# Second normalisation: the last token half's mean from row sums of the down weights and the gated values, its variance from squares summed by bank on ScalarE

## The chip, the cores and the metric

The kernel runs on one core of a Trainium2 chip. The metric is the device time of one execution in microseconds. A core has TensorE (PE), VectorE (DVE), ScalarE (ACT) and GpSimd (POOL), each with its own stream of instructions that it runs in order, and DMA queues fed from SyncE and GpSimd. The engines wait for one another by semaphores.

## The reference

A decoder layer over 256 tokens of 1024 features: a mixer, a normalisation, a gated MLP with a short convolution, and a second normalisation, which is the subject here.

```python
def layer_norm(x, g, b):
    xf = x.astype(jnp.float32)
    mu = xf.mean(-1, keepdims=True)
    var = jnp.square(xf - mu).mean(-1, keepdims=True)
    return ((xf - mu) * lax.rsqrt(var + LN_EPS) * g + b).astype(x.dtype)

def conv_gated_mlp(x, w_up, conv_ffn, w_down):
    u = causal_dwconv(jnp.einsum("bsd,df->bsf", x, w_up), conv_ffn)
    g, up = jnp.split(u, 2, axis=-1)
    return jnp.einsum("bsf,fd->bsd", jax.nn.silu(g) * up, w_down)
...
        x = layer_norm(ALPHA * x + mix, ln1_g[l], ln1_b[l])
        ffn = conv_gated_mlp(x, w_up[l], conv_ffn[l], w_down[l])
        x = layer_norm(ALPHA * x + ffn, ln2_g[l], ln2_b[l])
```

D_FF is 2816, that is 22 tiles of 128 features (NF). All is float32 to the outside.

## The kernel before

**Precision.** Each matrix product is made of three TensorE products. `split_into` (L87) cuts an operand into a high part (a cast on ScalarE, L89) and the rest (a subtraction on VectorE, L90); high times high, high times low and low times high are added up in PSUM.

**Order.** `chunk_order` lists the weight chunks (128x2048 each, one DMA each); `run` goes through them in that order. At step s it runs `elem_work` (L417): the evacuation left by step s-1, and in the places marked `None` of that list (or behind it) the halves of the split of the weights of step s+2. Then it starts a load, and issues the matmuls of step s. Every engine's stream is thus written out by hand: what stands in it is not moved by a scheduler. The MLP's steps are up 0 to 3, then dn 0, up 4, up 5, dn 1, up 6, up 7 and so on to dn 7, up 18, up 19, and at the end up 20, up 21, dn 8, dn 9, dn 10.

**An up step** gives one gated tile i of 128 features by 256 tokens. Its evacuation has two parts (`up_evac`). `conv` scales the result on ScalarE (L1104, two instructions) and adds the two older taps on VectorE (L1108, four). `gate` applies Silu on ScalarE (L1115), multiplies on VectorE (L1116), and splits the product into hh (L89, ScalarE) and hl (L90, VectorE). The list is `[conv, None, None, gate]`, so the two halves of a weight split stand between `conv` and `gate` on both engines. `up 0` and `up 1` are done token by feature and transposed back; their evacuation stands with that of up 2.

**A down step** dn d uses the gated tiles 2d and 2d+1 against the weight rows of the same features and adds into PSUM banks: for token half 0 two banks of 512 columns, for token half 1 one of 512 (bank 0) and two of 256 (banks 1 and 2). Steps 0 to 7 do both halves. Step dn 8 does all the rest of token half 0 (tiles 16 to 21, in this order), dn 9 bank 0 of half 1, dn 10 banks 1 and 2 (L1160 to L1171). A down step leaves no evacuation before dn 8.

**The second normalisation.** For each bank `ln_part` (L1000) adds the residual on VectorE (L1004) into the tile r of this token half and takes the statistics of it (`bn_stats`, L1005). For half 0 `ln_scale` makes mean and variance (L1013), and GpSimd raises the variance to -1/2 (L1014); `ln2_out` centres and multiplies by the gain (L1180), then scales and adds the bias (L1185) in two pieces of 512 columns, each followed by its DMA to the output. For half 1 this is in `finish` (L1188): the statistics are aggregated on VectorE (L1192), ScalarE takes the root (L1193; its table is loaded ahead of time at L1173), beside it VectorE centres (L1180), then takes the reciprocal (L1182) and does the last two passes.

Of the kernel before, what the change touches and what calls it, by code (L numbers as in the profile page):

```python
# [69 lines left out]
class Kernel:  # L70
# [1021 lines left out]
    def up_evac(self, i, get_ps):  # L1092
# [18 lines left out]
        def gate():  # L1111
            cu = st["cu"]
            hh = pp.tile([P, S], F32R, tag="hh", name=f"hh{i}", bufs=6)
            hl = pp.tile([P, S], F32R, tag="hlo", name=f"hl{i}", bufs=6)
# [1 line left out]
            v.tensor_mul(cu[:, 0, :], cu[:, 0, :], cu[:, 1, :])  # L1116
# [4 lines left out]
        return [conv, gate]

    def step_dn(self, s, d, *a):
        if d == 0:
# [6 lines left out]
        def mm(dd, kk, t, ps, cols):  # L1131
# [10 lines left out]
            for i, (left, right) in enumerate(((hh, wh), (hh, wl), (hl, wh))):  # L1142
                for lo, hi in parts[i]:
                    self.nc.tensor.matmul(ps[:, lo - a:hi - a], left, right[:, lo:hi], start=k == i == 0,  # L1144
                                          stop=k == NF - 1 and i == 2)

        def part(t, q):
            ps, cols = self.acc[t][q]
            self.ln_part(self.st[t], self.x1[:, t, :], ps, cols)
# [26 lines left out]
    def ln2_out(self, t):
        nc, st = self.nc, self.st[t]
        r, mv, rs = st["r"], st["mv"], st["rs"]
        v, (gain, bias) = nc.vector, self.lnrow
        v.scalar_tensor_tensor(r, r, mv[:, 0:1], gain, op0=ALU.subtract, op1=ALU.mult)  # L1180
        if t == 1:
            v.reciprocal(rs, rs)  # L1182
# [95 lines left out]
```

## Time and profile before

| what | value |
|---|---|
| median of 3 runs | 483.68 us (483.47 to 484.09) |
| the profiled execution's own time | 483.75 us |
| its span, first to last instruction | 481.9 us |
| instructions | 9733 |
| start of the MLP's first matmuls of dn 0 | 316.76 us |
| start of the last matmul | 474.51 us |
| start of the last pass of VectorE | 477.41 us |
| last output DMAs (two), issued from | 478.19 us |

Times in the traces count from the span's start. A row of the timeline has the start, the length, the engine, the line, the operation, output and inputs, and a count; rows of equal instructions are merged, so that the length of a merged row runs from the first start to the last end. In brackets stands idle time of the engine just before, and what ended it. A row of the view by groups has the busy time, the mean length in ns, and the idle time before. The names in it are those of the program's tiles: `raw` a chunk of weights as loaded, `wh` and `wl` its two parts, `cu` an up step's working tile, `ffn` the down product's banks, `ps_up` an up step's result.

### The profile page before, as it was taken

The page shows a single profiled execution, that of the slowest core. Times are in us where ns is not written, and L with a number is a line of the kernel's source. Part 1 is how long each engine was busy: PE and PEld are TensorE (multiplying, and loading weights), DVE is VectorE, ACT ScalarE, POOL GpSimd, SP SyncE. Part 2 cuts the span into 40 slices and gives each one's busy share as a digit, 9 for nine tenths or more (in the row PEclk, how much of TensorE's full clock was granted, in tenths as well). Part 3 has the DMA queues.
Part 4 walks back from the last instruction along what each step waited for, and adds up shares of the span by engine and source line. Part 5 has one row for each costly group of instructions (what it writes and reads, how often), then busy time and mean ns, then how long its engine had stood idle before and what let it go on. Part 6 is the DMA issues. An engine that isn't in the chain of part 4 may idle for free.

```text
span 481.9 us, 9733 instructions
## 1 busy us (share of the span) xinstructions
PE 473.1 (98%) x4016; PEld 464.8 (96%) x4016; DVE 368.9 (77%) x663; ACT 287.6 (60%) x487; POOL 30.2 (6%) x45
## 2 busy tenths in 40 slices
PE   8999999999999999999999999999999999999994
PEld 5999999999999999999999998999999999999993
DVE  4889985769676977785877788988768766776876
ACT  5686866585758665865764622767456544654540
POOL 0610011010100010002000001000000000000000
PEclk9999999999999999999999999999999999999998
DMA  7967646625663456424964491827464545455202
GB/s 262 386 253 210 216 176 211 260 89 174 222 234 126 141 217 235 164 94 175 356 252 174 179 346 34 308 97 262 175 218 175 209 186 192 173 214 209 88 1 87
DMA packets 18749, 93.76 MB, mean 195 GB/s; under 512 B 4593, under 2 KB 4857, under 8 KB 8849
## 3 DMA queue, kind: packets, MB, share of 16 engines
q1 hardware_dynamic: 14402, 86.82, 49.2%
q0 software_dynamic: 4160, 6.07, 4.2%
q8 instruction: 31, 0.51, 0.4%
q10 hardware_dynamic: 144, 0.26, 0.2%
q14 instruction: 12, 0.10, 0.1%
HBM read 92.05 MB, written 2.63 MB: 196 GB/s over the span
## 4 chain that ended last, share of the span: by engine, by line
PE 97%; DMA 1%; DVE 1%; SPq 0%; DVEq 0%; ACT 0%; issue 0%
PE ffn L1144 12%; PE ps_up L116 8%; PE ps_up L118 8%; PE ps_up L117 8%; PE ps_vm L116 2%; PE ps_vm L117 2%; PE ps_vm L118 2%; PE mix L118 2%; PE ps_wa L116 2%; PE ps_wb L116 2%; PE ps_ga L117 2%; PE ps_qb L116 2%; PE ps_gb L117 2%; PE ps_vb L117 2%; PE ps_qm L117 2%; PE ps_ga L116 2%
## 5 line engine op out<-in xcount | busy, mean ns | idle before, releaser
L90 DVE TENSOR_TENSOR wl<-raw,wh 128x1024 fp32r<-128x1024 f32 x150 | 176.6, 1220 | 28.2 <-ACT wh L89 28.1
L89 ACT CAST wh<-raw 128x1024 fp32r<-128x1024 f32 x150 | 149.6, 1052 | 4.6 <-DMA raw<-in_wst_dram 3.0
L117 PE MATMUL ps_up<-x1l,wh 128*128 128x256 f32 x320 | 88.3, 276 | 0.0
L118 PE MATMUL ps_up<-x1h,wl 128*128 128x256 f32 x320 | 88.3, 276 | 0.0
L116 PE MATMUL ps_up<-x1h,wh 128*128 128x256 f32 x319 | 88.1, 276 | 0.0
L117 PEld LDWEIGHTS ps_up<-x1l,wh 128*128 128x128 f32 x320 | 60.1, 188 | 0.0
L118 PEld LDWEIGHTS ps_up<-x1h,wl 128*128 128x128 f32 x320 | 60.1, 188 | 0.0
L116 PEld LDWEIGHTS ps_up<-x1h,wh 128*128 128x128 f32 x319 | 59.9, 188 | 0.0
L1108 DVE SCALAR_TENSOR_TENSOR cu<-ps_up,vec,cu 128x255 f32<-128x255 f32 (+1 forms) x80 | 33.0, 476 | 22.8 <-ACT cu L1104 22.8
L1144 PE MATMUL ffn<-wl,hh 128*128 128x256 f32 (+1 forms) x170 | 37.9, 280 | 0.0
L1144 PE MATMUL ffn<-wh,hl 128*128 128x256 f32 (+1 forms) x171 | 37.9, 280 | 0.0
L1144 PE MATMUL ffn<-wh,hh 128*128 128x256 f32 (+1 forms) x171 | 37.8, 279 | 0.0
L89 ACT CAST hh<-cu 128x256 fp32r<-128x256 f32 x22 | 8.9, 407 | 43.2 <-DVE cu L1116 43.2
L1104 ACT ACTIVATE cu<-ps_up,vec 128x256 f32<-128x256 f32 x40 | 16.7, 470 | 25.1 <-PE ps_up L118 25.1
L1144 PEld LDWEIGHTS ffn<-wh,hh 128*128 128x128 f32 x171 | 27.6, 188 | 0.3
L1144 PEld LDWEIGHTS ffn<-wh,hl 128*128 128x128 f32 x171 | 27.6, 188 | 0.3
L1144 PEld LDWEIGHTS ffn<-wl,hh 128*128 128x128 f32 x170 | 27.5, 188 | 0.2
L116 PE MATMUL mix<-wh,mgh 128*128 128x256 f32 x64 | 17.8, 279 | 0.0
L1014 POOL TENSOR_TENSOR rs<-mv,mhalf 128x1 f32<-128x1 f32 x3 | 3.0, 1000 | 235.7 <-DVE mv L1013 235.7
L117 PE MATMUL ps_vm<-wl,xth 128*128 128x256 f32 x64 | 17.8, 278 | 0.0
L116 PE MATMUL ps_qb<-xth,wh 128*128 128x256 f32 x64 | 17.8, 277 | 0.0
L116 PE MATMUL ps_wa<-yah,wh 128*128 128x256 f32 x64 | 17.8, 277 | 0.0
(312 smaller groups left out, 1439.1 us busy)
## 6 DMA issues: line engine op xcount, KB each, us to landing
raw<-in_wst_dram SPq DMA_DIRECT2D x77, 1024.0 KB, 4.9
rawr<-in_wst_dram SPq DMA_DIRECT2D x9, 256.0 KB, 5.7
lnrow<-in_rows_dram POOLq DMA_DIRECT2D x4, 512.0 KB, 6.0
rawr<-in_wst_dram SPq DMA_DIRECT2D x3, 512.0 KB, 5.6
band<-table POOLq DMA_DIRECT2D x4, 384.0 KB, 13.7
toe<-band POOLq DMA_DIRECT2D x4, 256.0 KB, 3.5
xtok<-in_x_dram POOLq DMA_DIRECT2D x1, 1024.0 KB, 5.2
out_dram<-r SPq DMA_DIRECT2D x4, 256.0 KB, 2.0
```

Of the source, the lines that this page charges most:

```text
L89: self.nc.scalar.copy(wh, raw)
L90: self.nc.vector.tensor_sub(wl, raw, wh.bitcast(F32))
L116: mm(ps, ah if first is None else first, bh, start=start, stop=False)
L117: mm(ps, ah, bl, start=False, stop=False)
L118: mm(ps, al, bh, start=False, stop=stop)
L1014: nc.gpsimd.tensor_tensor(st["rs"], st["mv"][:, 1:2], self.mhalf[:, 0:1], op=ALU.pow)
L1104: act.activation(cu[:, j, :], ps[:, j, :], AF.Copy, scale=tap(2, j))
L1108: v.scalar_tensor_tensor(cu[:, j, o:], ps[:, j, :S - o], tap(t, j), cu[:, j, o:], op0=ALU.mult, op1=ALU.add)
L1144: self.nc.tensor.matmul(ps[:, lo - a:hi - a], left, right[:, lo:hi], start=k == i == 0, stop=k == NF - 1 and i == 2)
```

## The change

The mean of a token over the 1024 outputs is known before the last matmul: the sum over columns of the down product is the sum over features of the gated value times the row sum of the down weights. The change computes token half 1's mean in this way.

- Each time the weights of a down step are split, ScalarE sums their rows: two ACTIVATE instructions (Copy, 128x1024, with an accumulator, `rows`), one for each of the two tiles of 128 features. Their output goes to the tile r of token half 0 (`st2[0]["r"]`) as scratch, the sums go to `wsum`. They are behind the evacuation list, so behind `gate` where the step before was an up step.
- The gated product is written to a tile of its own, `hf` (six buffers), not in place into `cu`. GpSimd multiplies its token half 1 by the row sum and adds it to `hsum` (`rowsum`; 22 products and 21 additions, 128x128).
- Behind bank 0 of token half 1 a small matmul adds `hsum` over the features (`ps_mu`, two columns). `x1_sum` sums the residual once on ScalarE and scales it on VectorE; `centre_known` puts the two together into the negative mean.
- For each bank `centre` adds the residual on VectorE, squares the centred values with an accumulator on ScalarE, and centres and multiplies by the gain on VectorE. The statistics (L1005, L1192) and the wide centring (L1180) of token half 1 are gone. `finish` adds up the first two banks' sums, takes the root with the third bank's sum as input and bias, and the reciprocal; the last passes are as before.

```diff
+        if self.order[s][0] == "dn":
+            d = self.order[s][1]
+            if d == 0:
+                self.st2 = [self.ln_tiles(f"2_{t}") for t in range(2)]
...
+            def rows():
+                for i, c in enumerate(cuts):
+                    k = 2 * d + i
+                    self.nc.scalar.activation(self.st2[0]["r"], c[2], AF.Copy, accum_out=self.wsum[:, k:k + 1])
+            return [lambda c=c: self.split_into(*c) for c in cuts] + [rows]
...
-            v.tensor_mul(cu[:, 0, :], cu[:, 0, :], cu[:, 1, :])
-            self.split_into(hh, hl, cu[:, 0, :])
+            hf = pp.tile([P, S], F32, tag="hf", name=f"hf{i}", bufs=6)
+            v.tensor_mul(hf, cu[:, 0, :], cu[:, 1, :])
+            self.split_into(hh, hl, hf)
+            self.hidf[i] = hf[:, P:]
...
+        def rowsum(dd):
+
+            for k in (2 * dd, 2 * dd + 1):
+                h, w = self.hidf.pop(k), self.wsum[:, k:k + 1].to_broadcast([P, P])
+                g.tensor_tensor(h if k else self.hsum, h, w, op=ALU.mult)
+                if k:
+                    g.tensor_tensor(self.hsum, self.hsum, h, op=ALU.add)
...
+            rowsum(d)
...
+            if d == 3:
+                self.evac[s] = self.x1_sum
...
             if d == d0 + 1:
-                self.nc.scalar.activation(self.st[1]["rs"], self.ident[:, 0:1], AF.Sqrt)
-                self.evac[s] = [lambda: part(1, 0)]
+                self.psmu = self.ps_main("ps_mu").rearrange("p a b -> p (a b)")[:, 0:2]
+                nc.tensor.matmul(self.psmu, self.hsum, self.mhalf, start=True, stop=True)
+                nc.scalar.activation(self.st[1]["rs"], self.ident[:, 0:1], AF.Sqrt)
+                self.evac[s] = [self.centre_known, lambda: self.centre(0)]
+
+    def x1_sum(self):
+        v, x = self.nc.vector, self.tiny[:, 0:1]
+        self.nc.scalar.activation(self.st[1]["r"], self.x1[:, 1, :], AF.Copy, scale=ALPHA, accum_out=x)
+        v.tensor_scalar(x, x, -1.0 / D, None, op0=ALU.mult)
+
+    def centre_known(self):
+
+        t = self.tiny
+        self.nc.vector.scalar_tensor_tensor(t[:, 1:2], self.psmu[:, 0:1], 2.0 / D, t[:, 0:1], op0=ALU.mult,
+                                            op1=ALU.add)
+
+    def centre(self, q):
...
+        v.scalar_tensor_tensor(r, self.x1[:, 1, c], ALPHA, ps, op0=ALU.mult, op1=ALU.add)
+        nc.scalar.activation(ps, r, AF.Square, bias=nmu, accum_out=sq)
+        v.scalar_tensor_tensor(st["r"][:, c], r, nmu, self.lnrow[0][:, c], op0=ALU.add, op1=ALU.mult)
...
     def finish(self):
-        for ps, cols in self.acc[1][1:]:
-            self.ln_part(self.st[1], self.x1[:, 1, :], ps, cols)
-        st = self.st[1]
-        self.nc.vector.bn_aggr(st["mv"], st["bs"][:, 0:st["n"], :].rearrange("p a b -> p (a b)"))
-        self.nc.scalar.activation(st["rs"], st["mv"][:, 1:2], AF.Sqrt)
+        nc, v, t, rs = self.nc, self.nc.vector, self.tiny, self.st[1]["rs"]
+        self.centre(1)
+        v.tensor_add(t[:, 5:6], t[:, 2:3], t[:, 3:4])
+        v.tensor_scalar(t[:, 5:6], t[:, 5:6], 1.0 / D, EPS, op0=ALU.mult, op1=ALU.add)
+        self.centre(2)
+        nc.scalar.activation(rs, t[:, 4:5], AF.Sqrt, scale=1.0 / D, bias=t[:, 5:6])
+        v.reciprocal(rs, rs)
         self.ln2_out(1)
```

Three places show what moves; line numbers of the changed kernel are its own (L1104 there is L1117, L1115 is L1128, L1004 is L1017). The numbers behind names tell buffers apart.

ScalarE's stream at the MLP's start, before: the copies of up 0 and up 1 for their way back, the cast of dn 0's weights (`wh_3859`), the convolutions of up 0 to up 2, Silu and the cast of the first gated tile.

```order
L1069 COPY tu<-ps_up_3778 128x2x256
L1069 COPY tu<-ps_up_3779 128x2x256
L89 CAST wh_3859<-raw_3722 128x1024 x2
L1104 ACTIVATE cu_3930<-ps_upT_3894,vec 128x256 x2
L1104 ACTIVATE cu_3937<-ps_upT_3899,vec 128x256 x2
L1104 ACTIVATE cu_3944<-ps_up_3869,vec 128x256 x2
L1115 ACT_TABLE_LOAD
```

ScalarE at the same place now:

```order
L1082 COPY tu<-ps_up_3779 128x2x256
L89 CAST wh_3859<-raw_3722 128x1024 x2
L121 ACTIVATE r_0_3861,wsum<-raw_3722 128x1024 x2
L1117 ACTIVATE cu_3943<-ps_upT_3907,vec 128x256 x2
L1117 ACTIVATE cu_3950<-ps_upT_3912,vec 128x256 x2
```

The pair of row sums stands between the cast of dn 0's weights and the first convolution.

ScalarE's stream at the MLP's end, before, from up 19's block to the root's table: `wh_5601`, `wh_5669` and `wh_5737` are the weights of dn 8, dn 9 and dn 10, and the three `hh` the gated tiles 19, 20 and 21.

```order
L89 CAST wh_5601<-raw_5424 128x1024 x2
L1115 ACTIVATE cu_5603<-cu_5603 128x256
L89 CAST hh_5614<-cu_5603 128x256
L1104 ACTIVATE cu_5671<-ps_up_5620,vec 128x256 x2
L89 CAST wh_5669<-raw_5480 128x1024 x2
L1115 ACTIVATE cu_5671<-cu_5671 128x256
L89 CAST hh_5682<-cu_5671 128x256
L1104 ACTIVATE cu_5739<-ps_up_5688,vec 128x256 x2
L89 CAST wh_5737<-raw_5550 128x1024 x2
L1115 ACTIVATE cu_5739<-cu_5739 128x256
L89 CAST hh_5750<-cu_5739 128x256
L1173 ACT_TABLE_LOAD
```

ScalarE at the same place now, from the cast of tile 19:

```order
L89 CAST hh_5685<-hf_5688 128x256
L121 ACTIVATE r_0_3861,wsum<-raw_5490 128x1024 x2
L1117 ACTIVATE cu_5745<-ps_up_5694,vec 128x256 x2
L89 CAST wh_5743<-raw_5550 128x1024 x2
L1128 ACTIVATE cu_5745<-cu_5745 128x256
L89 CAST hh_5756<-hf_5759 128x256
L121 ACTIVATE r_0_3861,wsum<-raw_5550 128x1024 x2
L1117 ACTIVATE cu_5816<-ps_up_5765,vec 128x256 x2
L89 CAST wh_5814<-raw_5621 128x1024 x2
L1128 ACTIVATE cu_5816<-cu_5816 128x256
L89 CAST hh_5827<-hf_5830 128x256
L121 ACTIVATE r_0_3861,wsum<-raw_5621 128x1024 x2
```

A pair of row sums follows the cast of each of the tiles 19, 20 and 21, and the next block's convolution stands behind the pair.

VectorE's stream at the very end, before, from the residual of token half 1's bank 0 (`ffn_4055`) on:

```order
L1004 SCALAR_TENSOR_TENSOR r_1_4049<-x_2995,ffn_4055 128x512
L1005 BN_STATS bs_1_4050<-r_1_4049 128x6
L1008 TENSOR_SCALAR bs_1_4050<-bs_1_4050 128x1
L1004 SCALAR_TENSOR_TENSOR r_1_4049<-x_2995,ffn_4056 128x256
L1005 BN_STATS bs_1_4050<-r_1_4049 128x6
L1004 SCALAR_TENSOR_TENSOR r_1_4049<-x_2995,ffn_4057 128x256
L1005 BN_STATS bs_1_4050<-r_1_4049 128x6
L1192 BN_AGGR mv_1_4051<-bs_1_4050 128x2
L1180 SCALAR_TENSOR_TENSOR r_1_4049<-r_1_4049,mv_1_4051,lnrow_4244 128x1024
L1182 RECIPROCAL rs_1_4052<-rs_1_4052 128x1
L1185 SCALAR_TENSOR_TENSOR r_1_4049<-r_1_4049,rs_1_4052,lnrow_4246 128x512 x2
```

VectorE at the same place now (`tiny` holds the negative mean and the sums):

```order
L1211 SCALAR_TENSOR_TENSOR tiny<-ps_mu,tiny 128x1
L1221 SCALAR_TENSOR_TENSOR res_5964<-x_2995,ffn_4064 128x512
L1223 SCALAR_TENSOR_TENSOR r_1_3865<-res_5964,tiny,lnrow_4260 128x512
L1221 SCALAR_TENSOR_TENSOR res_6004<-x_2995,ffn_4065 128x256
L1223 SCALAR_TENSOR_TENSOR r_1_3865<-res_6004,tiny,lnrow_4260 128x256
L1239 TENSOR_TENSOR tiny<-tiny 128x1
L1240 TENSOR_SCALAR tiny<-tiny 128x1
L1221 SCALAR_TENSOR_TENSOR res_6010<-x_2995,ffn_4066 128x256
L1223 SCALAR_TENSOR_TENSOR r_1_3865<-res_6010,tiny,lnrow_4260 128x256
L1243 RECIPROCAL rs_1_3868<-rs_1_3868 128x1
L1233 SCALAR_TENSOR_TENSOR r_1_3865<-r_1_3865,rs_1_3868,lnrow_4262 128x512 x2
```

The statistics give way to a centring of each bank as it comes, and the pass over all 1024 columns behind the last bank is gone. Ahead of these rows token half 0 is as before; its first instruction (L1017) writes `r_0_3861`, the tile into which the row sums of ScalarE write, and waits for TensorE and for ScalarE.

More of the change, by code (lines that the diff above doesn't have):

```diff
@@ L109, in split_parts @@
         self.w[s] = (wh, wl)
+        if self.order[s][0] == "dn":
+            d = self.order[s][1]
+            if d == 0:
+                self.st2 = [self.ln_tiles(f"2_{t}") for t in range(2)]
+                self.wsum = self.fp.tile([P, 64], F32, name="wsum")
+                self.hsum = self.fp.tile([P, P], F32, name="hsum")
+                self.tiny = self.fp.tile([P, 64], F32, name="tiny")
+            def rows():
[3 more added lines that the diff above has]
+            return [lambda c=c: self.split_into(*c) for c in cuts] + [rows]
         return [lambda c=c: self.split_into(*c) for c in cuts]
@@ L1045, in step_up @@
         if i == 0:
-            self.hid = {}
+            self.hid, self.hidf = {}, {}
             self.pt_up = [self.ps_side([P, 2, S], f"ps_up0{t}") for t in range(2)]
@@ L1123, in step_dn @@
     def step_dn(self, s, d, *a):
+        nc, g = self.nc, self.nc.gpsimd
         if d == 0:
-            self.st = [self.ln_tiles(f"2_{t}") for t in range(2)]
+            self.st = self.st2
             a0 = [self.ps_side([P, 512], f"ffn0{h}") for h in range(2)]
@@ L1143, in mm @@
                 for lo, hi in parts[i]:
[L1144 to L1149, printed above, removed]
+                    nc.tensor.matmul(ps[:, lo - a:hi - a], left, right[:, lo:hi], start=k == i == 0,
+                                     stop=k == NF - 1 and i == 2)
+        def rowsum(dd):
[4 more added lines that the diff above has]
+                    g.tensor_tensor(self.hsum, self.hsum, h, op=ALU.add)
         d0 = NF // 2 - 3
         if d < d0:
+            rowsum(d)
             for kk in range(2):
@@ L1162, in step_dn @@
         if d == d0:
+            for i in range(3):
+                rowsum(d0 + i)
             for k in ks:
@@ L1165, in step_dn @@
                     mm(*k, 0, *q)
-            self.evac[s] = [lambda: part(0, 0), lambda: part(0, 1), lambda: self.ln_scale(self.st[0]),
-                            lambda: self.ln2_out(0)]
+            self.evac[s] = [lambda q=q, c=c: self.ln_part(self.st[0], self.x1[:, 0, :], q, c) for q, c in self.acc[0]]
+            self.evac[s] += [lambda: self.ln_scale(self.st[0]), lambda: self.ln2_out(0)]
         else:
@@ L1172, in step_dn @@
             if d == d0 + 1:
-                self.nc.scalar.activation(self.st[1]["rs"], self.ident[:, 0:1], AF.Sqrt)
-                self.evac[s] = [lambda: part(1, 0)]
+                self.psmu = self.ps_main("ps_mu").rearrange("p a b -> p (a b)")[:, 0:2]
[11 more added lines that the diff above has]
+    def centre(self, q):
+        nc, v, st, t = self.nc, self.nc.vector, self.st[1], self.tiny
+        ps, cols = self.acc[1][q]
+        c = slice(*cols)
+        r = self.fp.tile([P, 2, S], F32, tag="cu", name=f"res{q}", bufs=3).rearrange("p a b -> p (a b)")
+        r = r[:, 0:c.stop - c.start]
+        nmu, sq = t[:, 1:2], t[:, 2 + q:3 + q]
+        v.scalar_tensor_tensor(r, self.x1[:, 1, c], ALPHA, ps, op0=ALU.mult, op1=ALU.add)
+        nc.scalar.activation(ps, r, AF.Square, bias=nmu, accum_out=sq)
+        v.scalar_tensor_tensor(st["r"][:, c], r, nmu, self.lnrow[0][:, c], op0=ALU.add, op1=ALU.mult)
     def ln2_out(self, t):
         nc, st = self.nc, self.st[t]
-        r, mv, rs = st["r"], st["mv"], st["rs"]
+        r, rs = st["r"], st["rs"]
         v, (gain, bias) = nc.vector, self.lnrow
-        v.scalar_tensor_tensor(r, r, mv[:, 0:1], gain, op0=ALU.subtract, op1=ALU.mult)
-        if t == 1:
-            v.reciprocal(rs, rs)
+        if t == 0:
+            v.scalar_tensor_tensor(r, r, st["mv"][:, 0:1], gain, op0=ALU.subtract, op1=ALU.mult)
         for h in range(2):
```

## The prediction

> **What bounds the kernel now.** I read the page first: the engine shares and the chain that ended last.
>
> ```profile
> PE 473.1 (98%) x4016; PEld 464.8 (96%) x4016; DVE 368.9 (77%) x663; ACT 287.6 (60%) x487; POOL 30.2 (6%) x45
> PE 97%; DMA 1%; DVE 1%; SPq 0%; DVEq 0%; ACT 0%; issue 0%
> ```
>
> TensorE is the bound, and 97% of the chain is its own work. The question for work added elsewhere is whether TensorE begins to wait. The view of waits, for TensorE alone, has two entries, both at the start:
>
> ```profile
> PE warm_ps L189 <- DVE warm L186: 1.2, 1, 1.2
> PE ps_o L149 <- ACT whr L89: 0.4, 1, 0.4
> ```
>
> So any later wait is new time. ScalarE's 60% and VectorE's 77% are averages; what counts is how early their products are ready where the order is tight. Two such places are read in the timeline: the first down-projection step, which uses the first two gated tiles, and step dn8, which ends with tile 21 (hid 21), the last one made. After the last matmul VectorE finishes alone; that tail is the third place.
>
> **The last gated tile.** ScalarE, timeline, blocks of up19 to up21 (start, length, engine, line):
>
> ```profile
> 452.77 0.41 ACT L89 CAST hh<-cu 128x256 fp32r<-128x256 f32 x1 [2.12 <-DVE cu L1116]
> 453.08 0.84 ACT L1104 ACTIVATE cu<-ps_up,vec 128x256 f32<-128x256 f32 x2
> 458.24 0.41 ACT L89 CAST hh<-cu 128x256 fp32r<-128x256 f32 x1 [2.13 <-DVE cu L1116]
> 458.55 0.84 ACT L1104 ACTIVATE cu<-ps_up,vec 128x256 f32<-128x256 f32 x2
> 459.28 2.00 ACT L89 CAST wh<-raw 128x1024 fp32r<-128x1024 f32 x2
> 463.71 0.41 ACT L89 CAST hh<-cu 128x256 fp32r<-128x256 f32 x1 [2.12 <-DVE cu L1116]
> ```
>
> A block runs from one convolution start (L1104) to the next: 458.55 - 453.08 = 5.47 us. The cast of hh comes 463.71 - 458.55 = 5.16 us into it, after a wait of 2.1 us for VectorE, and the next convolution starts 0.31 us after that cast began, with no idle time of its own. So ScalarE is idle in each block, but ahead of hh; between hh and the next convolution there is no gap. The order rows put the new row sums just there. VectorE's side of the last block and its consumer on TensorE:
>
> ```profile
> 459.42 1.65 DVE L1108 SCALAR_TENSOR_TENSOR cu<-ps_up,vec,cu 128x255 f32<-128x255 f32 x4 [0.32 <-ACT cu L1104]
> 460.99 2.35 DVE L90 TENSOR_TENSOR wl<-raw,wh 128x1024 fp32r<-128x1024 f32 x2
> 464.15 0.43 DVE L90 TENSOR_TENSOR hl<-cu,hh 128x256 fp32r<-128x256 f32 x1 [0.47 <-ACT hh L89]
> 463.69 0.39 PE L1144 MATMUL ffn<-wh,hh 128*128 128x256 f32 x2
> 465.05 0.39 PE L1144 MATMUL ffn<-wh,hh 128*128 128x512 f32 x1
> 465.51 0.39 PE L1144 MATMUL ffn<-wh,hl 128*128 128x512 f32 x1
> ```
>
> The matmuls of tile 20 start at 463.69, those of tile 21 at 465.05 (hh) and 465.51 (hl). hh21 is ready at 463.71 + 0.41 = 464.12, which leaves 0.93 us; hl21 at 464.58 leaves 0.93 too.
>
> **The price of a row sum.** It is an ACTIVATE over 128x1024 with an accumulator. The nearest rows:
>
> ```profile
> L89 ACT CAST wh<-raw 128x1024 fp32r<-128x1024 f32 x150 | 149.6, 1052 | 4.6 <-DMA raw<-in_wst_dram 3.0 <-ACT sga L920 1.6
> L814 ACT ACTIVATE lg<-lg,mx 128x256 f32<-128x256 f32 x8 | 4.0, 496 | 0.0
> L814 ACT ACTIVATION_READ_ACCUMULATOR lg<-lg,mx 128x1 f32 x16 | 3.0, 188 | 0.0
> ```
>
> The same size costs 1.05 us, and the softmax's accumulating ACTIVATE is followed by a read of the accumulator, 0.19 us. Two casts in a row take 2.00 us (459.28), so starts lie 0.95 apart; I add 0.10 for a read that overlaps in the same way. The two sums of a pair write the same scratch tile, so the second waits for the first to end: another 0.14 (the full 0.19 instead of 0.10, and 0.05 for the signal, an estimate). A pair: 2 x (0.95 + 0.10) + 0.14 = **2.24 us**. Lower end: accumulators free, 1.90. Upper end: nothing overlaps, 2 x (1.05 + 0.19 + 0.05) = 2.58.
>
> In steps 1 to 7 the pair comes in the slot after a down step, where no gated tile stands behind it and ScalarE waits for TensorE, as in the last of these slots:
>
> ```profile
> 442.13 0.84 ACT L1104 ACTIVATE cu<-ps_up,vec 128x256 f32<-128x256 f32 x2 [3.38 <-PE ps_up L118]
> ```
>
> A pair of 2.24 fits into 3.38; x1_sum adds one 1.05 us there once, 3.3 in all. I cost these at nothing. If the cover were gone, the gated tiles made behind them would still lie a down step and two blocks ahead of their use.
>
> **Sum at dn8.** The pair for dn8 moves up20's convolution from 453.08 to 455.32. That for dn9 moves up21's to 455.32 + 5.47 + 2.24 = 463.03. hh21 then starts at 468.19 and ends at 468.60, and TensorE starts tile 21 at 468.64 where it did at 465.05: **3.59 us later**. Tile 20 doesn't hide it: its wl half is ready at 460.99 + 1.18 + 4.48 = 466.65, and its remaining ten matmuls (1.1 us) end by 467.9. hl21 follows hh21 as before and just makes its slot.
>
> **Sum at dn0.** ScalarE and VectorE where the first gated tiles are made, and TensorE's first use of tile 1:
>
> ```profile
> 305.67 2.00 ACT L89 CAST wh<-raw 128x1024 fp32r<-128x1024 f32 x2
> 308.35 1.57 ACT L1104 ACTIVATE cu<-ps_upT,vec 128x256 f32<-128x256 f32 x4 [0.67 <-PE ps_upT L1076]
> 312.40 1.65 DVE L1108 SCALAR_TENSOR_TENSOR cu<-ps_up,vec,cu 128x255 f32<-128x255 f32 x4
> 314.13 0.43 DVE L1116 TENSOR_TENSOR cu<-cu 128x256 f32<-128x256 f32 x1
> 318.71 0.41 ACT L89 CAST hh<-cu 128x256 fp32r<-128x256 f32 x1 [1.50 <-DVE cu L1116]
> 319.53 0.39 PE L1144 MATMUL ffn<-wh,hh 128*128 128x256 f32 x2
> ```
>
> The pair stands between the cast and the convolutions: 307.57 + 2.24 = 309.81 instead of 308.35, 1.46 late. VectorE's twelve taps run without a gap and pass it on, less the 0.08 between 314.05 and 314.13. hh1, ready at 319.12 with 0.41 to spare, comes 1.38 late at 320.50; TensorE takes it at 320.54 for 319.53: **1.0 us**. Everything behind moves with it.
>
> **Sum of the tail.** VectorE and TensorE at the end:
>
> ```profile
> 465.95 0.69 DVE L1004 SCALAR_TENSOR_TENSOR r<-x,ffn 128x512 f32<-128x512 f32 x1 [1.37 <-PE ffn L1144]
> 467.40 0.15 DVE L1008 TENSOR_SCALAR bs<-bs 128x1 f32<-128x1 f32 x1
> 472.22 0.68 DVE L1004 SCALAR_TENSOR_TENSOR r<-x,ffn 128x512 f32<-128x512 f32 x1
> 473.74 0.41 DVE L1004 SCALAR_TENSOR_TENSOR r<-x,ffn 128x256 f32<-128x256 f32 x1
> 474.83 0.42 DVE L1004 SCALAR_TENSOR_TENSOR r<-x,ffn 128x256 f32<-128x256 f32 x1 [0.21 <-PE ffn L1144]
> 476.01 1.28 DVE L1180 SCALAR_TENSOR_TENSOR r<-r,mv,lnrow 128x1024 f32<-128x1024 f32 x1
> 477.21 0.16 DVE L1182 RECIPROCAL rs<-rs 128x1 f32<-128x1 f32 x1
> 477.41 1.41 DVE L1185 SCALAR_TENSOR_TENSOR r<-r,rs,lnrow 128x512 f32<-128x512 f32 x2
> 470.54 0.28 PE L1144 MATMUL ffn<-wh,hh 128*128 128x256 f32 x1
> ```
>
> From the first token half's start (465.95) to the second's (472.22) VectorE needs 6.27 us, the same instructions after. But its first instruction writes the tile r_0 into which the row sums write their scratch, so it must wait for dn10's pair too: that starts 0.31 behind hh21, at 468.50, and ends 2.34 later (2.24 and the last overlap), at 470.84; TensorE's bank would be there at 469.54. So 470.87, and the second half starts at 477.14, 4.92 late. From there, by the rows: L1211 0.07, 512 wide 0.72 and 0.64, bank 1's pair 0.44 and 0.40: 479.41. The two tiny ones wait for ScalarE's sum of bank 1, which starts at 479.0, 0.50 and a read 0.10: they run from 479.64 to 479.88. Bank 2's residual then ends at 480.30, its squares with read at 480.92, Sqrt (0.25) 481.2, reciprocal 0.20, and L1233 starts at 481.42 for 477.41: **4.0 us** late, of which the shorter tail has given back 0.9. The last two passes and their DMAs are unchanged.
>
> GpSimd's sums and the small matmul are hidden: for the last pair two operations follow 470.84. No elementwise row has their form; the nearest are these, 0.41 to 0.86, and I take the one of the same shape.
>
> ```profile
> L298 POOL CAST xfirst<-xth 128x128 fp32r<-128x128 f32 x1 | 0.9, 857 | 0.0
> L713 POOL TENSOR_SCALAR_AFFINE_SELECT wt<-wt 128x256 f32<-128x256 f32 x4 | 1.6, 409 | 104.0 <-ACT wt L712 104.0
> ```
>
> They end by 472.6, while TensorE comes to ps_mu at 470.54 + 3.59 = 474.1; the cover is gone above 1.6 us each. The matmul itself (bounds 0.1 and 1) delays bank 2 to 479.5 at worst, before VectorE asks at 479.88.
>
> Total: 1.0 + 4.0 = 5.0 us on the profiled execution's own 483.75 (span 481.9 and 1.85 around it): **488.8**. That execution lies 0.07 above the median. Three pairs and the one at dn0 enter, so the pair's ends (1.90, 2.58) give 487.4 and 490.2.
>
> **Rivals.** *The row sums hide in ScalarE's wait, not slower.* For it: 2.1 us idle per block against a pair of 2.24. The place is dn8, the price the 4.0 there; it turns when two pairs fit in hh21's 0.93 us, that is below 0.47 us a pair, or when the pair ran ahead of hh, which the order rows exclude. Then the tail's gain of 0.9 is left, bounded by the last bank (474.83 and ps_mu) to some 0.75: 483.0, with dn0 hidden too.
>
> *Only TensorE is delayed, and r_0 is no wait*: if the pair behind hh21 ends before bank 0, or isn't waited for. Then 3.59 + 1.0 less 0.85 in the shorter tail: 487.5.
>
> *GpSimd and VectorE collide at dn0.* GpSimd's product of tile 1 starts with ScalarE's cast of hh1, and hl1 on VectorE comes 0.45 later; a product of 0.86 that held VectorE off would make hl1 0.4 late and add 0.4: 489.2. [...] No row here shows the two at once.
>
> *TensorE loses its clock in the new waits.* The windows of the tail show it falling to half after the last matmul:
>
> ```profile
> 478.00:479.00 1.00, 0.00 (x0) 0.00 (x0) 0.82 (x2) 0.00 (x0) 0.00 (x0) 1.00 0.00 0
> 479.00:480.00 1.00, 0.00 (x0) 0.00 (x0) 0.00 (x0) 0.00 (x0) 0.00 (x0) 0.52 0.98 371
> ```
>
> TensorE's last result released VectorE at 474.83 and the clock falls just behind 479.0: some 4.2 us of idleness. The waits at dn8 are three pieces of about 1.2, 1.6 and 0.8 us. If they counted together, one such stretch at half clock loses 2.1 us, so bank 2 is done at 474.83 + 3.59 + 2.1 = 480.5 where VectorE asks at 479.88: 489.4, and 491.5 for two. [...]
>
> **How the numbers follow.** Chances: forecast 0.64; hidden 0.08; no wait for r_0 0.10; collision 0.10; clock 0.08. The range reaches from a cheap pair without most of the r_0 wait to a dear pair or a lost clock: 486.9 to 490.5. A measurement of this kernel can tell about 0.2%, 1 us. Hidden splits into same 0.05 and faster 0.03; all the others are slower, 0.92.
>
> **What would show it.** In the changed profile: TensorE waits at L1160 (its line there) for hh or wl near dn8, 3.6 us in all, and 1.0 at dn0; the convolution starts of up20 and up21 7.7 us apart; VectorE's first L1017 of the tail released by ScalarE; from the end of hh21's cast to the start of the last passes 12.8 us where it was 13.3. Wrong would make it a pair below 1.9 us, TensorE without waits, or a row sum that runs during ScalarE's wait.

## The result, and the profile after

| kernel | executions | median | lowest to highest | ratio to before, 95% |
|---|---|---|---|---|
| before | 6 | 483.90 us | 483.47 to 484.58 | 1 |
| changed | 6 | 488.56 us | 488.19 to 494.49 | 1.0133 [1.0104, 1.0162] |

The change makes the kernel 4.7 us slower; the forecast was 488.8. The six executions fall into two groups, four at 488.2 to 488.6 and two at 494.4 to 494.5. The profiled one, at 494.49 us with a span of 492.7, is of the long group. The same kernel was therefore profiled again (experiment e5), in an execution of 489.05 us with a span of 487.3; what is said of the usual execution is read from that one.

The page of the changed kernel, engine shares and the chain that ended last:

```profile
PE 482.5 (98%) x4018; PEld 473.0 (96%) x4018; DVE 368.1 (75%) x664; ACT 315.7 (64%) x539; POOL 49.1 (10%) x88
PE 91%; DVE 4%; ACT 3%; issue 1%; DVEq 0%
```

ScalarE has 28 us more work and TensorE's part of the chain fell from 97% to 91%: VectorE and ScalarE now stand in it. The waits of TensorE in the usual execution (total, times, longest; a fifth entry, 0.2 us, lies at the kernel's start):

```profile
PE ffn L1160 <- DVE wl L90: 1.4, 1, 1.4
PE warm_ps L202 <- DVE warm L199: 1.2, 1, 1.2
PE ffn L1160 <- ACT hh L89: 1.2, 2, 0.7
PE ffn L1160 <- ACT wh L89: 1.0, 1, 1.0
```

Where there was no wait in the MLP, there are four at L1160. TensorE's timeline of the usual execution shows one of 0.68 us at dn0 and three at dn8:

```profile
319.31 0.28 PE L1160 MATMUL ffn<-wh,hl 128*128 128x256 f32 x1
320.26 0.50 PE L1160 MATMUL ffn<-wh,hh 128*128 128x256 f32 x2 [0.68 <-ACT hh L89]
320.61 0.40 PE L1160 MATMUL ffn<-wl,hh 128*128 128x256 f32 x2
...
464.32 0.39 PE L1160 MATMUL ffn<-wh,hl 128*128 128x256 f32 x2
465.67 0.50 PE L1160 MATMUL ffn<-wh,hh 128*128 128x256 f32 x2 [0.96 <-ACT wh L89]
467.56 0.50 PE L1160 MATMUL ffn<-wl,hh 128*128 128x256 f32 x2 [1.39 <-DVE wl L90]
467.89 0.39 PE L1160 MATMUL ffn<-wh,hl 128*128 128x256 f32 x2
...
468.57 0.39 PE L1160 MATMUL ffn<-wh,hl 128*128 128x256 f32 x2
469.46 0.64 PE L1160 MATMUL ffn<-wh,hh 128*128 128x512 f32 x1 [0.50 <-ACT hh L89]
469.90 0.63 PE L1160 MATMUL ffn<-wl,hh 128*128 128x512 f32 x1
```

A wait costs what it adds to the distance of two starts. At dn0 single matmuls start 0.11 us apart, and here 0.95: 0.84 lost. Pairs of 256 columns (and single ones of 512) start 0.23 apart, but the pair right behind this wait is 0.35 ahead of the next, which makes 0.96 in all. At dn8 the three gaps are 1.35, 1.89 and 0.89, so 3.44 lost, and with the 0.33 behind the second of them 3.54. The last two rows are 0.44 apart where 0.23 is usual. The windows of this execution show what goes with that (length; busy time and count of PE, PEld, DVE, ACT, POOL; granted clock; DMA share; GB/s):

```profile
462.60:469.60 7.00, 4.15 (x32) 3.55 (x31) 4.41 (x8) 4.84 (x11) 1.73 (x4) 1.00 0.00 0
469.60:473.20 3.60, 3.60 (x12) 3.00 (x13) 1.73 (x5) 3.50 (x6) 1.72 (x4) 0.53 0.00 0
```

In the 7 us of the three waits TensorE was busy for 4.15 at full clock; behind them it got about half the clock for 3.60 us, which loses 3.60 x 0.47 = 1.7 us. ScalarE, timeline of the same execution, from the cast of tile 20's hh (hh20) to up21's convolution, and at hh21:

```profile
461.31 0.41 ACT L89 CAST hh<-hf 128x256 fp32r<-128x256 f32 x1 [2.12 <-DVE hf L1130]
461.62 1.06 ACT L121 ACTIVATE r<-raw 128x1024 f32<-128x1024 f32 x1
462.58 0.19 ACT L121 ACTIVATION_READ_ACCUMULATOR r<-raw 128x1 f32 x1
462.80 1.06 ACT L121 ACTIVATE r<-raw 128x1024 f32<-128x1024 f32 x1
463.77 0.18 ACT L121 ACTIVATION_READ_ACCUMULATOR r<-raw 128x1 f32 x1
463.86 0.82 ACT L1117 ACTIVATE cu<-ps_up,vec 128x256 f32<-128x256 f32 x2
...
469.01 0.40 ACT L89 CAST hh<-hf 128x256 fp32r<-128x256 f32 x1 [2.13 <-DVE hf L1130]
```

The pair takes 463.86 - 461.62 = 2.24 us and stands behind the cast; the idle 2.12 us ahead of the cast is still there. VectorE, timeline of the tail, usual execution:

```profile
471.68 0.69 DVE L1017 SCALAR_TENSOR_TENSOR r<-x,ffn 128x512 f32<-128x512 f32 x1 [1.80 <-ACT r L121]
...
477.62 0.15 DVE L1211 SCALAR_TENSOR_TENSOR tiny<-ps_mu,tiny 128x1 f32<-128x1 f32 x1
...
480.38 0.15 DVE L1240 TENSOR_SCALAR tiny<-tiny 128x1 f32<-128x1 f32 x1
481.14 0.42 DVE L1221 SCALAR_TENSOR_TENSOR res<-x,ffn 128x256 f32<-128x256 f32 x1 [0.60 <-PE ffn L1160]
...
482.75 1.42 DVE L1233 SCALAR_TENSOR_TENSOR r<-r,rs,lnrow 128x512 f32<-128x512 f32 x2
```

The first row waits for ScalarE's last row sum, as forecast. But the last bank's residual then waits 0.60 us for TensorE: at this place the matmuls that ran late and at half clock decide, and VectorE waits for them.

**The long group.** Windows over the middle of the MLP, the profiled long execution of the changed kernel:

```profile
330.00:345.00 15.00, 15.00 (x130) 15.00 (x129) 11.66 (x19) 10.72 (x19) 1.89 (x4) 1.00 0.60 211
394.00:411.00 17.00, 17.00 (x146) 17.00 (x146) 11.76 (x19) 11.13 (x19) 1.89 (x4) 1.00 0.50 188
```

The first of these in the usual execution:

```profile
330.00:345.00 15.00, 15.00 (x135) 15.00 (x134) 11.66 (x19) 10.72 (x19) 1.85 (x4) 1.00 0.59 209
```

VectorE and ScalarE did the same work, and TensorE was never idle, but in the long execution it did 130 matmuls where the usual one did 135, at a granted clock of 1.00 in both. TensorE's rows in the long execution, at the dn0 wait, 9 us later and where it ends:

```profile
319.62 0.28 PE L1160 MATMUL ffn<-wl,hh 128*128 128x256 f32 x1
319.73 0.28 PE L1160 MATMUL ffn<-wh,hl 128*128 128x256 f32 x1
320.69 0.50 PE L1160 MATMUL ffn<-wh,hh 128*128 128x256 f32 x2 [0.68 <-ACT hh L89]
...
330.10 0.28 PE L130 MATMUL ps_up<-x1l,wh 128*128 128x256 f32 x1
330.22 0.28 PE L131 MATMUL ps_up<-x1h,wl 128*128 128x256 f32 x1
...
482.07 0.28 PE L1199 MATMUL ps_mu<-mhalf,hsum 128*128 128x2 f32 x2
...
482.64 0.28 PE L1160 MATMUL ffn<-wh,hh 128*128 128x256 f32 x1
482.75 0.28 PE L1160 MATMUL ffn<-wl,hh 128*128 128x256 f32 x1
```

Each matmul is as long as before (0.28), but from the dn0 wait on they start 0.12 us apart, until the small matmul of ps_mu at 482.07; then 0.11 again. Five of 135 over the 161 us between these two points is 6.0 us; the two groups lie 494.4 - 488.5 = 5.9 apart. No step of the prediction had this slow pitch. The spacing itself is not new: the kernel before has it too, at another place and without a wait, for instance from 51.00 to 56.30 us (45 steps of 0.118 on `ps_vm`), and the profiled long execution of the changed kernel has it there too (51.08 to 56.38 us, 45 steps of 0.118).

### The profile page after: what moved, and what is told of

It reads as the page before. It is cut to its first block, busy times and chain, and to the rows that moved or that the text cites. A ratio compares the mean times of both kernels' runs of the same rounds, so it can differ in the third digit from the quotient of the medians.

```text
span 492.7 us, 9852 instructions
## 1 busy us (share of the span) xinstructions
PE 482.5 (98%) x4018; PEld 473.0 (96%) x4018; DVE 368.1 (75%) x664; ACT 315.7 (64%) x539; POOL 49.1 (10%) x88
## 4 chain that ended last, share of the span: by engine, by line
PE 91%; DVE 4%; ACT 3%; issue 1%; DVEq 0%
PE ffn L1160 11%; PE ps_up L129 7%; PE ps_up L131 7%; PE ps_up L130 7%; DVE cu L1121 2%; DVE wl L90 2%; PE ps_vm L129 1%; PE ps_vm L130 1%; PE ps_vm L131 1%; PE mix L129 1%; PE ps_wa L129 1%; PE ps_wb L129 1%; PE ps_vb L131 1%; PE ps_qm L131 1%; PE ps_ga L131 1%; PE ps_gb L131 1%
## 5 line engine op out<-in xcount | busy, mean ns | idle before, releaser
L130 PE MATMUL ps_up<-x1l,wh 128*128 128x256 f32 x320 | 89.8, 281 | 0.0
L131 PE MATMUL ps_up<-x1h,wl 128*128 128x256 f32 x320 | 89.8, 281 | 0.0
L129 PE MATMUL ps_up<-x1h,wh 128*128 128x256 f32 x319 | 89.6, 281 | 0.0
L131 PEld LDWEIGHTS ps_up<-x1h,wl 128*128 128x128 f32 x320 | 61.3, 192 | 0.0
L1160 PE MATMUL ffn<-wh,hh 128*128 128x256 f32 (+1 forms) x171 | 39.7, 291 | 1.5 <-ACT hh L89 1.2
L1160 PE MATMUL ffn<-wl,hh 128*128 128x256 f32 (+1 forms) x170 | 39.3, 288 | 1.4 <-DVE wl L90 1.4
L1160 PE MATMUL ffn<-wh,hl 128*128 128x256 f32 (+1 forms) x171 | 39.0, 287 | 0.0
L89 ACT CAST hh<-hf 128x256 fp32r<-128x256 f32 x22 | 8.9, 406 | 44.1 <-DVE hf L1130 44.1
L1160 PEld LDWEIGHTS ffn<-wh,hh 128*128 128x128 f32 x171 | 28.4, 191 | 2.4 <-ACT hh L89 1.6
L1160 PEld LDWEIGHTS ffn<-wl,hh 128*128 128x128 f32 x170 | 28.2, 192 | 1.8 <-DVE wl L90 1.6
L1160 PEld LDWEIGHTS ffn<-wh,hl 128*128 128x128 f32 x171 | 28.5, 192 | 0.4
L1167 POOL TENSOR_TENSOR hf<-hf,wsum 128x128 f32<-128x128 f32 x21 | 9.8, 465 | 139.2 <-ACT r L121 134.2
L1117 ACT ACTIVATE cu<-ps_up,vec 128x256 f32<-128x256 f32 x40 | 16.7, 469 | 10.7 <-PE ps_up L131 10.1
L121 ACT ACTIVATE r<-raw 128x1024 f32<-128x1024 f32 x22 | 23.3, 1058 | 0.3
```

Of the source, the lines that this page charges most:

```text
L89: self.nc.scalar.copy(wh, raw)
L121: self.nc.scalar.activation(self.st2[0]["r"], c[2], AF.Copy, accum_out=self.wsum[:, k:k + 1])
L129: mm(ps, ah if first is None else first, bh, start=start, stop=False)
L130: mm(ps, ah, bl, start=False, stop=False)
L131: mm(ps, al, bh, start=False, stop=stop)
L1117: act.activation(cu[:, j, :], ps[:, j, :], AF.Copy, scale=tap(2, j))
```

## The experiments

Four things were open: whether the order on ScalarE is the whole cause of the loss (the forecast's theory); whether the wait for the scratch tile r_0 costs anything beside TensorE's lost clock (the rival on the clock); whether the collision of GpSimd and VectorE has a part; and what puts TensorE into the slow pitch. A "pair" is the two row sums of one down step.

The first four experiments move pairs (e1 to e3) or add one to the kernel before (e4). In e1 to e3 the sums of some steps leave the end of the evacuation list. At dn0 one sum stands between the convolutions of up1 and up2 and the other behind tile 1's Silu; at dn8 to dn10 both stand behind Silu, ahead of the cast of hh, where ScalarE waits for VectorE.

```diff
-            return [lambda c=c: self.split_into(*c) for c in cuts] + [rows]
+            halves = [lambda c=c: self.split_into(*c) for c in cuts]
+            if d == 0 or d >= 8:
+                self.rows = [lambda i=i: row(i) for i in range(2)]
+                return halves
+            return halves + [lambda: (row(0), row(1))]
...
-            parts = [a0, a1, conv, b0, None, None, b1, gate]
+            parts = [a0, a1, lambda: self.rows.pop(0)(), conv, b0, None, None, b1, gate]
...
             act.activation(cu[:, 0, :], cu[:, 0, :], AF.Silu)
+            if i == 1 or i >= 19:
+                for f in self.rows:
+                    f()
+                self.rows = []
```

This is e3, with both moves; `row(i)` is one of the two ACTIVATE instructions. In e1 the conditions are `d == 0` and `i == 1`; in e2 they are `d >= 8` and `i >= 19`, without the edit of `parts`.

### e1: only dn0's pair moved

> Only the pair of row sums of dn 0 moves: the first sum stands between the convolutions of up 1 and up 2, where ScalarE waited 1.6 us for TensorE, the second behind Silu of tile 1, where it waited 1.5 us for VectorE. Theory (the pair ahead of the convolutions makes hh1 late, and TensorE's wait there of about 1.0 us also starts the slower pitch of its matmuls, 118 ns apart instead of 113, in the executions near 494.4): TensorE has no wait at dn 0, the usual executions come to 487.4 us (1.0 below the changed kernel's usual 488.4), and none lies near 493. Rival (the slow pitch comes from something else in the change, such as GpSimd's work): 487.4 in most, and about a third near 493.4 again.

Measured: 488.06 us median of 4 (487.76 to 488.36), before 483.93; 1.0081 [1.0068, 1.0095]. There is no wait at dn0 and no long execution. The median is 0.5 us below the changed kernel's usual group and not 1.0: the expected 487.4 is missed by 0.7. In the two profiles the 1.0 is there when the time is counted from dn0's first matmul to the start of the last passes: 482.06 - 316.94 = 165.12 us here, 482.75 - 316.64 = 166.11 in the usual execution of the changed kernel. How early dn0 starts differs from execution to execution (316.64 to 317.94 in the profiles), so a difference of half a microsecond between medians of four and eight executions says little.

### e2: only the pairs of dn8 to dn10 moved

> Only the pairs of dn 8, dn 9 and dn 10 move, from behind the cast of hh to between Silu and that cast, where ScalarE waits 2.1 us for VectorE. Theory (the pairs behind hh make the last tiles 3.6 us late, and r_0 holds VectorE up): no wait of TensorE at dn 8, VectorE's half 0 released by TensorE, usual executions at 484.0 us (483.75, 1.0 at dn 0, 0.8 less in the tail), others near 489.9 where the slow pitch starts at dn 0. Rival (a pair costs the same wherever it stands, since ScalarE is short of time): 487 to 488.5.

Measured: 484.34 us median of 11 (483.81 to 489.90); 1.0022 [0.9994, 1.0050]. Nine lie at 483.8 to 484.7 with a median of 484.21, two at 489.9. TensorE's waits, all of them:

```profile
PE warm_ps L205 <- DVE warm L202: 1.2, 1, 1.2
PE ffn L1167 <- ACT hh L89: 0.7, 1, 0.7
```

Only dn0's wait is left, and with it the long executions.

### e3: both moved

> Both moves together. Theory: TensorE waits nowhere in the MLP, and the shorter tail alone is left: 483.0 us, 0.8 below the kernel before, no slow executions. Rival (the tail gives nothing, since the small matmul, the squares on ScalarE and the tiny operations take the place of the statistics): 483.7 to 484.2.

Measured: 483.24 us median of 11 (482.90 to 483.87); 0.9985 [0.9977, 0.9994]. ScalarE and then VectorE, timelines of this kernel at hh21 and at the end:

```profile
461.21 0.42 ACT L1131 ACTIVATE cu<-cu 128x256 f32<-128x256 f32 x1
461.52 1.06 ACT L119 ACTIVATE r<-raw 128x1024 f32<-128x1024 f32 x1
...
463.96 0.41 ACT L89 CAST hh<-hf 128x256 fp32r<-128x256 f32 x1
...
475.10 0.42 DVE L1228 SCALAR_TENSOR_TENSOR res<-x,ffn 128x256 f32<-128x256 f32 x1 [0.27 <-PE ffn L1167]
...
476.71 1.41 DVE L1240 SCALAR_TENSOR_TENSOR r<-r,rs,lnrow 128x512 f32<-128x512 f32 x2
```

The pair now fills the stretch between Silu and the cast. The wait of 2.1 us ahead of the cast is gone, and the cast starts at 463.96, only 0.25 us later than before the change, which the 0.93 us of reserve takes in. TensorE has no wait in the MLP and there was no long execution. What is left of the change is its gain: the last passes start at 476.71 instead of 477.41, 0.7 us earlier, and the median is 0.7 us lower. So the same sums, at other places of the same stream, cost TensorE nothing, and the dn0 pair costs 484.21 - 483.24 = 0.97 us (usual executions), the end pairs 488.06 - 483.24 = 4.82. This version is faster than the kernel before by 0.7 us, a small difference that the interval just sets apart from none, and faster than the changed kernel by 5.3.

### e4: the kernel before, with dn0's pair alone

The pair writes a scratch of its own and its sums are not used.

```diff
+        if self.order[s] == ("dn", 0):
...
+                    self.nc.scalar.activation(scr, c[2], AF.Copy, accum_out=wsum[:, i:i + 1])
+            return [lambda c=c: self.split_into(*c) for c in cuts] + [rows]
```

> The kernel before with one thing added: the pair of row sums of dn 0, ahead of the convolutions as in the change, with a scratch tile of its own and its sums not used. Theory: TensorE waits about 1.0 us at tile 1 of dn 0: 484.8 us in the usual executions, and in some of them the matmuls from there on are 118 ns apart instead of 113 to the end, which gives about 490.7. Rival (the slow pitch belongs to GpSimd's work or to the dn 8 waits): 484.8 in all executions.

Measured: 489.17 us median of 10, in two groups: 484.75 to 485.90 (four) and 490.66 to 491.00 (five), with one at 487.68; 1.0094 [1.0060, 1.0128]. Its one MLP wait:

```profile
PE ffn L1152 <- ACT hh L89: 0.7, 1, 0.7
```

GpSimd's products, the waits of dn8 and the new tail are not in this kernel. The pair at dn0 with its wait of 0.7 us is enough for the long executions. That they run at the slow pitch is inferred from their distance to the others: the traces kept of long executions are those of the changed kernel and of e6.

### e5: the changed kernel again

> The changed kernel once more, for the profile of an execution without the slow pitch if one is caught, and for the shares. Theory: most executions at 488.2 to 488.6 us, with matmuls 113 ns apart between dn 0 and dn 8, some at 494.4 with 118. In an execution of the first kind TensorE waits 0.7 to 1.0 us at dn 0 and about 3.6 at dn 8, and L1233 of half 1 starts about 4 to 4.6 us later than in the kernel before beyond the wait at dn 0.

Measured: 488.23, 488.56, 489.05, 489.90, 493.47 and 493.61 us, before 483.99; 1.0131 [1.0096, 1.0167]. With the first six, 8 of 12 executions are usual ones and 4 are long. The rows are shown above: TensorE lost 0.96 us at dn0 and 3.54 at dn8, and the last passes start 482.75 - 477.41 = 5.34 us later than before, 4.4 beyond what dn0 lost.

### e6: the changed kernel, row sums to a scratch of their own

```diff
-                    self.nc.scalar.activation(self.st2[0]["r"], c[2], AF.Copy, accum_out=self.wsum[:, k:k + 1])
+                    self.nc.scalar.activation(self.scr, c[2], AF.Copy, accum_out=self.wsum[:, k:k + 1])
```

> Only the tile changes into which the row sums write: one of their own instead of token half 0's r. Theory of the forecast (VectorE's wait for r_0 costs): L1017 of half 0 is released by TensorE, up to 1.3 us earlier, and the time falls by 0.9 to 487.5. Rival (TensorE's clock has halved behind the waits at dn 8, so its last bank comes later than VectorE's work and the r_0 wait lies beside it): within 0.3 us of the changed kernel, 488.1 to 488.6, with the last residual released by TensorE.

Measured: 487.77, 490.29, 492.70, 494.42, 494.87 and 495.47 us; 1.0163 [1.0121, 1.0205]. The times are inconclusive: the dn0 wait is still in this kernel, most executions are long, and a difference below 1 us can't be read from them. The profile, of the execution of 494.87 us, has the releases that the rival expected: the first residual waits 1.28 us for TensorE and no longer for ScalarE, and the last one still 0.60 us for TensorE. The times went to e9.

### e7: e4, with a small matmul behind dn0

The slow pitch ended at the small matmul of ps_mu. If such a matmul ends it, one behind dn0 removes the long group.

```diff
+            if d == 0:
+                psx = self.ps_main("ps_x").rearrange("p a b -> p (a b)")[:, 0:2]
+                self.nc.tensor.matmul(psx, self.ident, self.mhalf, start=True, stop=True)
```

> As the fourth experiment (kernel before plus the pair of dn 0), and behind dn 0's matmuls one small float32 matmul like ps_mu (128x2, result not used). The slow pitch of the changed kernel's profiled execution ended at ps_mu. Theory (such a matmul ends the slow pitch): no execution near 491, all at 484.8 to 486. Rival (its end at ps_mu was chance, or needs something else): about half near 490.9 again.

Measured: 486.23 us median of 10: six at 484.98 to 486.52 and four at 490.54 to 490.92; 1.0079 [1.0046, 1.0112]. TensorE in the profiled one (485.82, of the short group), behind the wait at dn0 and on both sides of the small matmul:

```profile
323.42 0.28 PE L1152 MATMUL ffn<-wh,hh 128*128 128x256 f32 x1
...
324.01 0.28 PE L1152 MATMUL ffn<-wh,hl 128*128 128x256 f32 x1
324.13 0.28 PE L1167 MATMUL ps_x<-mhalf,ident 128*128 128x2 f32 x2
...
325.06 0.28 PE L124 MATMUL ps_up<-x1h,wh 128*128 128x256 f32 x1
...
326.99 0.28 PE L126 MATMUL ps_up<-x1h,wl 128*128 128x256 f32 x1
```

Five steps of 0.118 us lie between the first two rows and seventeen of 0.1135 between the last two: in this execution the slow pitch began behind the wait and was over behind the small matmul. But the long group is still there, so a small matmul behind dn0 doesn't keep an execution out of it. No long execution of this kernel was profiled, so whether the slow pitch goes on there or starts again is open. What ends it stays open.

### e8: the kernel before, with the pairs of dn8 to dn10 alone

The condition of e4 is `in (("dn", 8), ("dn", 9), ("dn", 10))`; the sums are not used, and the tail is the old one.

> The kernel before with the pairs of dn 8, dn 9 and dn 10 behind the cast of hh as in the change, with a scratch tile of their own and the sums not used; the tail is that of before. Theory: TensorE waits 3.6 us in all at dn 8, so 487.4 us if its clock holds; where the granted clock falls to half for one stretch of about 3.4 us behind these waits, 1.7 more, 489.0. Rival (the lateness at dn 8 is hidden by the rest of the tail): 484.5 or less.

Measured: 487.40, 488.68, 488.92 and 489.46 us; 1.0093 [1.0077, 1.0109]. The mean granted clock of these four, in that order, is 0.997, 0.991, 0.994 and 0.992: the one with the most clock meets the expectation for a kept clock (487.4), the others the one for a lost clock (489.0). One stretch of 3.4 us at half clock, as the changed kernel's profile has it (0.50 from 474.70 to 478.10 us), takes 0.0035 off the mean of such a span. That leaves 0.9965 even where nothing else is lost, so the execution at 0.997 can hardly have had a whole one. The other three means prove nothing alone: the halved clock behind the last matmul (0.50 to 0.52 behind 479.0 us in the kernel before) counts too, and the kernel before itself runs from 0.994 to 0.998. No execution is long. VectorE in the profiled one:

```profile
480.62 0.42 DVE L1012 SCALAR_TENSOR_TENSOR r<-x,ffn 128x256 f32<-128x256 f32 x1 [1.24 <-PE ffn L1152]
```

There is no wait for r_0 in this kernel, and its last residual waits 1.24 us for TensorE.

### e9: e1, with the scratch of e6

> The first experiment (pair of dn 0 moved, no wait and no slow pitch there) with a scratch tile of its own for the row sums, so that the wait for r_0 is asked once more without the slow pitch. Theory of the forecast: 1.3 us earlier for VectorE's half 0, of which up to 0.9 reach the end: 487.1 against the first experiment's 488.06. Rival (with the clock halved behind the waits at dn 8 TensorE's last bank decides, and the r_0 wait lies beside it): 487.9 to 488.2, and only executions whose clock held (granted clock 0.997 or more) near 486.8.

Measured: 487.96 us median of 5 (487.64 to 488.94), before 484.12; 1.0082 [1.0069, 1.0096], against 1.0081 for e1. VectorE, first and last residual of the tail:

```profile
470.57 0.69 DVE L1021 SCALAR_TENSOR_TENSOR r<-x,ffn 128x512 f32<-128x512 f32 x1 [1.28 <-PE ffn L1168]
...
480.08 0.42 DVE L1229 SCALAR_TENSOR_TENSOR res<-x,ffn 128x256 f32<-128x256 f32 x1 [0.60 <-PE ffn L1168]
```

VectorE no longer waits for ScalarE, and the median is only 0.1 us below that of e1: the last residual waits 0.60 us for TensorE, as with the shared scratch. So the wait for r_0 is real, but it is not what the end pairs cost. One part of the rival's expectation failed: the execution with a mean granted clock of 0.998, which can't have had a whole stretch at half clock, took 488.05 us and not about 486.8. No trace of it was kept, and what it lost instead is open. In the profiled execution the clock falls at about 467.6 us (its mean is 0.95 from 464 to 468 us and 0.62 from 468 to 472), behind two waits of 0.95 and 1.39 us, and TensorE's wait for hh21 is gone: the slower matmuls ahead of it fill that time.

## Why the prediction was right, and which steps were not

**The price of a pair** was 2.24 us, and is 2.24. The 0.05 for the signal in it was the author's estimate; in the row the second sum starts 0.03 behind the first one's read (462.80, after 462.58 + 0.19). **hh21** was to start 5.16 us behind up21's convolution, and both late by two pairs, with the convolutions of up20 and up21 7.7 us apart; they start 463.86 - 456.17 = 7.69 apart, and hh21 starts at 469.01, 5.15 behind 463.86. The forecast's 468.19 and the 0.96 lost at dn0, less the 0.12 by which this execution reaches dn0 earlier (316.64, before 316.76), make 469.03.

**dn0** was to lose 1.0 us on TensorE; TensorE lost 0.96 there and the median 0.97 (e2 against e3). **dn8** was to make tile 21 3.59 us late; it lost 3.54. Both were shown by removal: with the pairs elsewhere (e3) the waits are gone and the time is 0.7 us below that of before. And by addition: the kernel before with one of them alone (e4, e8) has the same waits.

**The wait for r_0**, which in the sum carried the path behind dn8, is the step that failed although the total came out. The row has it (1.80 us, released by ScalarE), but e9 takes it away and gains 0.1 us in the median. The path runs over TensorE: late by the waits, then at half clock. The forecast had bank 2 ready before VectorE asked for it; in the usual execution VectorE was done with the tiny ones at 480.38 + 0.15 = 480.53 and had to wait until 481.14. The last passes start at 482.75, 0.33 us behind the forecast's 482.42 (481.42 and the 1.0 of dn0); from the end of hh21's cast (469.41) it is 13.34 us and not 12.8.

**The rival on the clock**, with a chance of 0.08, is therefore the one that happened: behind three waits with matmuls between them the granted clock was 0.53 over 3.60 us. Its price was to be 0.6 us above the forecast, with 2.1 us lost at half clock; the loss was 1.7, and the last bank by the rival's sum with 1.7 in the place of 2.1 and the 1.0 of dn0, 474.83 + 3.59 + 1.7 + 1.0 = 481.1, is where the row has it. All six profiles with the waits at dn8 show the clock halved behind them: 0.50 to 0.53 over 2.0 to 3.6 us in the changed kernel, e5, e1 and e6, and 0.62 and 0.66 over 4.0 us that hold the stretch in e9 and e8. Without them the kernel before has 1.00 up to the last matmul, and e2's mean of 0.999 leaves no room for such a stretch. That the forecast's total still fits is in part luck: the path that it took through r_0 was nearly as long as the one that decided, 480.53 against 481.14, and without the 1.7 us VectorE would have been the later of the two.

The windows say how long it lasted and what stood ahead of it. In the long execution of the changed kernel the clock was 0.50 from 474.70 to 478.10 us, and in the usual one the share lost gives the same length, 3.60 x 0.47 x 2 = 3.4 us; in e1 it is 3.50 x 0.48 x 2 = 3.4. TensorE was busy ahead of it for 4.15 of 7.00 us in the usual execution, 4.18 of 7.00 in e1, and from 464 to 468 us 1.66 of 4.00 in e8 and in e9 (in e9 the last 0.4 of them at half clock). The one wait of 0.68 us at dn0 left the clock at 1.00 (changed kernel, 316 to 330 us, busy for 13.32 of 14.00). How much idleness it takes, and whether the length of a single wait counts or how the waits fall, is not shown.

**The tail** was to give back 0.75 to 0.9 us; in e3, where nothing else is late, it gives 0.7. The changed kernel has this gain too: from the last bank's residual to the last passes it takes 482.75 - 481.14 = 1.61 us, and before it took 477.41 - 474.83 = 2.58, so 0.97 less. Of that the small matmul takes back 0.22: counted from dn0's first matmul, the last residual of e3 starts 158.29 us behind it and that of before 158.07. With this the whole loss adds up, counted from dn0's first matmul to the last passes: 0.96 (dn0) + 3.54 (dn8) + 1.7 (clock) + 0.22 (small matmul) - 0.97 (tail) = 5.45, measured 166.11 - 160.65 = 5.46.

**The collision of GpSimd and VectorE at dn0** had a wrong premise, and its product of 0.86 us took 0.52 there. GpSimd and VectorE around tile 1 in the profiled execution of the changed kernel:

```profile
321.18 0.52 POOL L1167 TENSOR_TENSOR hf<-hf,wsum 128x128 f32<-128x128 f32 x1 [4.52 <-DVE hl L90]
321.77 0.46 POOL L1169 TENSOR_TENSOR hsum<-hsum,hf 128x128 f32<-128x128 f32 x1
321.90 0.61 DVE L90 TENSOR_TENSOR hl<-hf,hh 128x256 fp32r<-128x256 f32 x1 [0.47 <-ACT hh L89]
```

The product writes over hf, so it can't start before VectorE has made hl1 from it; it starts behind, and the two can't meet there. One tile later they do: the subtraction that overlaps GpSimd's addition lasts 0.61 us instead of the 0.43 of the prediction's rows, without anyone waiting for it. In e3 a like overlap goes with most of the 0.25 us by which the cast of hh21 is later: VectorE's product of tile 21 (from 463.30) takes 0.62 us there instead of 0.42, beside a product of GpSimd (from 462.75) that takes 0.89 instead of 0.40.

**The long group** was in no step. It goes with dn0's wait: of the kernels with that wait (changed, e2, e4, e7; e6, whose times don't fall apart into two groups, left aside) 15 of 43 executions are long, of those without it (e1, e3, e8, e9) none of 24, and of the kernel before none of the 51 run beside the experiments (highest 486.83). A wait alone is not what it takes: e1, e3 and e8 have waits of 0.8, 0.6 and 0.7 us at the kernel's start (`ps_o`) and no long execution. And behind the stretch at half clock the profile of e9 runs at 0.118 us too, without a wait at dn0 (from 471.34 to 474.88 us, fifteen pairs 0.236 apart, where e1 has 0.228 from 472.53 to 473.67); over these pairs it costs about 0.1 us, 15 x (0.236 - 0.228), an estimate from the spacing. The long group doesn't touch the sign, since the usual group alone is 4.7 us slower, and the predicted range (486.9 to 490.5) holds the median; it doesn't hold the long executions.

## What to carry to other kernels

On an engine that runs in order, ask where its idle time stands in the stream: the 2.1 us ahead of a cast were useless to work placed behind that cast, and free to the same work placed ahead of it; this move and the one at dn0 together turned a loss of 4.7 us into a gain of 0.7. Where the engine that bounds the kernel runs without a break, as TensorE in this MLP, a few short waits cost more than their length here, through the clock (1.7 us at dn8) and in some executions through the pitch (5.9 us behind dn0), so a place where no wait arises was worth more than the length of the wait says. Work added for a shorter tail has to be counted at every place where it is issued, not at the tail alone.
